# Softmax rows scaled after the values' products, the first attention operands loaded inside the projection phase, and the output projection interleaved with the norm behind it

## The chip, the cores and the metric

The kernel runs on one core of a Trainium2 chip. The metric is the device time of one execution in microseconds (us). Inputs and outputs lie in the chip's memory (HBM); they and nearly all products are float32. A float32 product is made of three TensorE products of rounded parts: each operand is split into a high part (a cast to fp32r) and a low part (the rest), and hi·hi, hi·lo and lo·hi are added in PSUM.

## The reference, cut to what matters

One layer of a streaming encoder, for 1024 prompt frames and for 64 sample frames that continue an older stream with 256 cached frames. Eight heads are RWKV-7 (a recurrence over a matrix state), eight are "FoX" heads: softmax attention with a bias made of running sums of forget gates.

```
mod = silu(c) @ w_ada + b_ada                    # 6 x 1024 columns per sequence
sh1, sc1, gt1, sh2, sc2, gt2 = split(mod, 6)
h    = rms_norm(x, norm1_g) * (1 + sc1) + sh1
proj = h @ w_in                                  # RWKV columns and FoX columns
...                                              # RWKV-7 scan, gate -> y_rwkv
s = einsum(q, k) * HEAD_DIM**-0.5 + (lc_q - lc_k)
p = softmax(where(causal, s, -inf))
y_fox = einsum(p, v)
x  = x + gt1 * (concat([y_rwkv, y_fox]) @ w_out)
h2 = rms_norm(x, norm2_g) * (1 + sc2) + sh2
x  = x + gt2 * ((silu(h2 @ w_ffn_gate) * (h2 @ w_ffn_up)) @ w_ffn_down)
```

Width 1024, 8 RWKV and 8 FoX heads of 64, FFN width 2816. Besides y, the last states, the keys, values and forget gates are outputs.

## The kernel before, in words

Activations stand with their features on the 128 partitions and the frames along the free axis. The frames are cut into two halves: half 0 has the first 512 prompt frames, half 1 the other 512 and the 64 of the sample, 576 in all. Weights come in slices of 128 output columns: `load_w` issues the load (512 KB, four buffers `wraw`), then casts the high part on ScalarE (`whi`) and subtracts the low part (`wlo`, L216) on GpSimd or VectorE. The flag `pool_lo` chooses which.

A scheduler of the framework sets the order of the instructions of each engine from the order in which the program issues them and from which data they need; each engine then runs its own queue strictly in order, and SyncE's queue issues nearly all DMAs.

The stages, by the times of the profile:

- 0 to 40: loads, the first 16 of 48 slices of the `w_ada` product.
- 40 to 680: `phase` for each half: the input projection, slice by slice (`pmm`, L294 to L296), and between the slices the steps of an order that is written out by hand, the string ORDER. Z, D, A, B and N belong to one pair of RWKV heads, Q, K, q, k, V, C and L to FoX heads. B (`rwkv_b`) inverts small triangular matrices (32x32 products, L523, L549), transposes (L567, L575) and then runs the scan, nine dependent steps of 64 frames (L597 to L618). The remaining 32 `w_ada` slices (`pada`, the list `background`) are spread over the projection's slices. Finished queries and keys go by DMA to scratch memory in HBM (`qx`, `kx`), values to `vscr`.
- In half 1, ORDER ends with "Q3 q3 K2 k3 k2 V3". B and N of the last head pair stand in no string; they are issued behind it (`late`).
- 714 to 820 and on to 940: attention, for half 0 and then half 1. `attend` first loads the head's operands from scratch (`qsx`, `k1x`, `q2x`, `k2x`, `vsx`, seven DMAs), then makes units of one or two tiles of 128 queries: scores (`psc`), mask, row maximum (`nm`), exponential with row sum (`p`, `ls`), reciprocal of `ls`, and the multiplication of `p` by it (one tile in three on ScalarE, L917, two on VectorE, L919). Then `p` is transposed (`ppt`), split in two (`pth`, `ptl`), multiplied with the values (`pav`), and the two halves of the partitions are added (`avt`, `fy`, L957 to L959). `Pipe(2)` keeps three units in flight, at different steps. Half 0 has 32 tiles in 16 units, half 1 has 40 tiles in 24 units.
- Between 820 and 940 the output projection of half 0 (`po`, eight slices of `w_out`) is issued between the units of half 1.
- 940 to 1040: first the norm of half 0 is finished and the first part of its FFN input made (`h2_make`, L1040 to L1045), with the output projection of half 1 behind it in program order; then the norm and `h2_make` of half 1. Its residual is L992, its squares L1000 and L1002.
- 1040 to 1490: the FFN's gate and up products (`fast_half`, L1143, seven products in place of eight of half size). From there to the end the down product (`pd`, L1244), which reads the gated activations back from scratch (`act_load`, buffer `as`), splits them (`ah`, `al`) and adds into x.

PSUM has eight banks. `pav` has one buffer in half 0 and in half 1.

Of the kernel before, what the change touches and what calls it, by code (L numbers as in the profile page):

```python
# [7 lines left out]
F32 = mybir.dt.float32  # L8
# [3 lines left out]
ALU = mybir.AluOpType  # L12
# [23 lines left out]
         "T3 Z0 D0 A0 L Z1 K0 D1 U3 B0 A1 D2 Z2 Q0 N0 k0 A2 q0 D3 Q1 B1 K1 q1 Z3 A3 k1 V2 N1 V1 B2 V0 Q2 q2 K3 N2 Q3 q3 K2 k3 k2 V3")  # L36
# [28 lines left out]
class K:  # L65
# [7 lines left out]
    def consts(self):  # L73
# [14 lines left out]
        self.ct = self.cmid.tile([P, KT, 32], F32, name="ct")  # L88
# [570 lines left out]
    def logf(self, hf):  # L659
# [43 lines left out]
        if hf.smp:  # L703
            order += [(5, True, SP, P, None), (6, False, SP + P, P, None), (4, False, SP + PAST, SS, SP)]
# [25 lines left out]
        for g in (order[0:4], order[4:]):  # L730
            if not g:
                continue
            if g[0][0] != 0:
                pr = self.ps([32, 4, P], tag="fx", name="plr")
                rows = self.slot([32, 4, P], F32R, name="lrow", tag="fx")
            for x, (i, _, _, m, _) in enumerate(g):
                nc.tensor.transpose(pr[:, x, 0:m], q4[0:m, i].rearrange("p a h -> p (a h)"), self.ident[0:m, 0:m])
            w = sum(m for _, _, _, m, _ in g)
            rf = rows.rearrange("r x t -> r (x t)")
            nc.vector.tensor_copy(rf[:, 0:w], pr.rearrange("r x t -> r (x t)")[:, 0:w])  # L740
            ck = g[0][2]
            x0, cq, wq = [(x, cq, 512 if x == 0 else m) for x, (_, _, _, m, cq) in enumerate(g) if cq is not None][0]
            for part in range(2):
                r = 16 + 8 * part
                nc.sync.dma_start(self.kx[:, 130 + part, ck:ck + w], rf[r:r + 8, 0:w].bitcast(F32))
                nc.sync.dma_start(self.qx[:, 128 + part, cq:cq + wq],
                                  rf[8 * part:8 * part + 8, x0 * P:x0 * P + wq].bitcast(F32))
# [38 lines left out]
    def put_split(self, src, j, t0, n, is_k):  # L786
# [5 lines left out]
        for x, r in ((hi, 0 if is_k else 64), (lo, 64 if is_k else 0)):  # L792
            m = min(n, 512)
            for h in range(2):
                t = (self.kx if is_k else self.qx)[2 * j + h, r:r + 64]
                hs = slice(64 * h, 64 * h + 64)
# [32 lines left out]
    def cache_kv(self, j):  # L829
# [6 lines left out]
        self.put_split(kf, j, SP, PAST, 1)  # L836
        self.put_v(j, vc, 8, 2, P)

    def att_pools(self, es, R):
# [13 lines left out]
        T2 = lambda name, shape: [ap.tile(shape, F32R, name=f"{name}x{i}") for i in range(2)]  # L853
        self.qs, self.q2 = T2("qs", [P, 640]), T2("q2", [68, 640])
        self.k1, self.k2 = T2("k1", [P, 1344]), T2("k2", [68, 1344])
        self.vs = T2("vs", [P, 11, P])
        for i in range(2):
            nc.gpsimd.memset(self.qs[i][:, 576:640].bitcast(F32), 0.0)
            nc.gpsimd.memset(self.q2[i][:, 576:640].bitcast(F32), 0.0)

    def attend(self, hd, hf):

        nc = self.nc
        j, h = hd // 2, hd % 2
        hs = slice(64 * h, 64 * h + 64)
        i2 = hd % 2
        qs, q2, k1, k2, vs = self.qs[i2], self.q2[i2], self.k1[i2], self.k2[i2], self.vs[i2]
# [12 lines left out]
        else:  # L880
            nc.sync.dma_start(vs[:, 0:4].bitcast(F32), self.vscr[hd][:, 0:4])
        if h == 0:
# [4 lines left out]
        def unit(qp):  # L887
# [4 lines left out]
            ptiles = []  # L892
            for t in range(1 if smp else 2):
# [13 lines left out]
                nc.tensor.matmul(pq[0:qn, nk - qn:nk], self.identb[0:qn, 0:qn], self.cmask[0:qn, 0:qn], start=False,  # L907
                                 stop=True, skip_group_check=True)
                nm = self.tpool.tile([P, 1], F32, tag="nm", name="nm")
                ls = self.tpool.tile([P, 1], F32, tag="ls", name="ls")  # L910
                nc.vector.tensor_reduce(nm[0:qn], pq[0:qn, 0:nk], axis=AX.X, op=ALU.max, negate=True)
                p = self.tpool.tile([P, 1024], F32, tag="p", name="p")
                nc.scalar.activation(p[0:qn, 0:nk], pq[0:qn, 0:nk], AF.Exp, bias=nm[0:qn], accum_out=ls[0:qn])
                nc.vector.reciprocal(ls[0:qn], ls[0:qn])
# [725 lines left out]
```

## Time and profile before

| | us |
|---|---|
| median of three runs | 1759.51 (1754.32 to 1764.12) |
| the profiled execution | 1761.91 |
| its span in the trace | 1760.2 |
| TensorE busy | 1673.6 (95%), mean granted clock 0.974 |
| VectorE busy | 1105.8 (63%) |
| ScalarE busy | 728.0 (41%) |
| GpSimd busy | 267.6 (15%) |

In the profile PE is TensorE, PEld its weight loads, DVE VectorE, ACT ScalarE, POOL GpSimd, SP SyncE, and SPq the issuing of DMAs on SyncE's queue. Lines such as L917 are lines of the kernel before. PEclk is the clock that TensorE was granted, 1.00 being full speed. A row of a stretch gives its bounds and length, then busy time and number of instructions for each engine, then PEclk, the DMA engines' busy share and GB/s. A row of a group gives line, engine, operation, output<-inputs, shape and number, then the sum of the busy time and the mean of one in ns, then the time for which the engine had sat idle ahead of them and what ended that.

### The profile page before, as it was taken

The page shows a single profiled execution, that of the slowest core. Times are in us where ns is not written, and L with a number is a line of the kernel's source. Part 1 is how long each engine was busy: PE and PEld are TensorE (multiplying, and loading weights), DVE is VectorE, ACT ScalarE, POOL GpSimd, SP SyncE. Part 2 cuts the span into 40 slices and gives each one's busy share as a digit, 9 for nine tenths or more (in the row PEclk, how much of TensorE's full clock was granted, in tenths as well). Part 3 has the DMA queues.
Part 4 walks back from the last instruction along what each step waited for, and adds up shares of the span by engine and source line. Part 5 has one row for each costly group of instructions (what it writes and reads, how often), then busy time and mean ns, then how long its engine had stood idle before and what let it go on. Part 6 is the DMA issues. An engine that isn't in the chain of part 4 may idle for free.

```text
span 1760.2 us, 33567 instructions
## 1 busy us (share of the span) xinstructions
PE 1673.6 (95%) x12893; PEld 1454.0 (83%) x12893; DVE 1105.8 (63%) x2518; ACT 728.0 (41%) x1532; POOL 267.6 (15%) x468
## 2 busy tenths in 40 slices
PE   5999999999999998889999779999999999999999
PEld 3676666688888886666888779999999999999998
DVE  6676676757786753777876685556666654444434
ACT  4435454543555344566776363233333222112110
POOL 2102121121222122100212300000000000222221
PEclk9999999999999997889999899999999999999999
DMA  8435356642233336376663302222222224533313
GB/s 314 151 87 157 116 165 195 184 122 71 76 75 92 107 84 167 96 203 166 158 188 128 106 34 83 74 74 74 74 74 78 79 89 134 182 99 93 99 36 120
DMA packets 136143, 207.10 MB, mean 118 GB/s; under 512 B 64687, under 2 KB 72911, under 8 KB 135983
## 3 DMA queue, kind: packets, MB, share of 16 engines
q1 hardware_dynamic: 135982, 204.95, 39.1%
q8 instruction: 102, 1.67, 0.4%
q14 instruction: 59, 0.48, 0.1%
HBM read 157.65 MB, written 47.25 MB: 116 GB/s over the span
## 4 chain that ended last, share of the span: by engine, by line
PE 81%; DVE 7%; ACT 6%; issue 3%; DMA 3%; POOL 1%; SPq 0%; ACTq 0%; DVEq 0%; POOLq 0%
PE pd L1244 15%; PE pfc L1143 7%; PE pfe L1143 7%; PE pfa L1143 7%; PE pmm L294 5%; PE pmm L296 5%; PE pmm L295 5%; PE pfb L1143 4%; PE pav L952 2%; PE pbs L375 2%; PE ppt L930 2%; PE pA L464 2%; PE pS L613 1%; PE po L295 1%; PE po L294 1%
## 5 line engine op out<-in xcount | busy, mean ns | idle before, releaser
L216 POOL TENSOR_TENSOR wlo<-wraw,whi 128x512 fp32r<-128x512 f32 (+2 forms) x64 | 107.1, 1675 | 777.5 <-ACT whi L212 772.2
L294 PE MATMUL pmm<-hhi,whi 128*128 128x288 f32 (+1 forms) x624 | 220.3, 353 | 1.0 <-ACT pb L317 0.7
L295 PE MATMUL pmm<-hlo,whi 128*128 128x288 f32 (+1 forms) x624 | 216.8, 347 | 1.4 <-DVE hlo L272 1.4
L296 PE MATMUL pmm<-hhi,wlo 128*128 128x288 f32 (+1 forms) x624 | 215.6, 345 | 0.0
L212 ACT CAST whi<-wraw 128x1024 fp32r<-128x1024 f32 (+2 forms) x116 | 99.2, 855 | 234.8 <-PE pd L1244 168.1
L1244 PE MATMUL pd<-ah,whi 128*128 128x512 f32 (+1 forms) x528 | 173.3, 329 | 2.2 <-ACT ah L212 2.2
L1244 PE MATMUL pd<-al,whi 128*128 128x512 f32 (+1 forms) x528 | 174.1, 330 | 0.5 <-DVE al L216 0.5
L1244 PE MATMUL pd<-ah,wlo 128*128 128x512 f32 (+1 forms) x528 | 173.7, 329 | 0.0
L1248 DVE SCALAR_TENSOR_TENSOR x1t<-pd,mod,x1t 128x512 f32<-128x512 f32 x192 | 90.6, 497 | 132.1 <-PE pd L1244 131.0
L294 PEld LDWEIGHTS pmm<-hhi,whi 128*128 128x128 f32 x624 | 119.2, 191 | 14.3 <-ACT pb L317 2.5
L295 PEld LDWEIGHTS pmm<-hlo,whi 128*128 128x128 f32 x624 | 119.4, 191 | 11.1 <-DVE hlo L272 2.1
L296 PEld LDWEIGHTS pmm<-hhi,wlo 128*128 128x128 f32 x624 | 119.4, 191 | 10.2 <-issue 1.2
L1143 PE MATMUL pfc<-hh,hS 128*128 128x256 f32 (+1 forms) x352 | 102.3, 291 | 8.0 <-ACT hh L1045 5.6
L1244 PEld LDWEIGHTS pd<-ah,whi 128*128 128x128 f32 x528 | 99.8, 189 | 10.5 <-ACT ah L212 2.7
L1244 PEld LDWEIGHTS pd<-al,whi 128*128 128x128 f32 x528 | 99.8, 189 | 8.5 <-DVE al L216 0.7
L1244 PEld LDWEIGHTS pd<-ah,wlo 128*128 128x128 f32 x528 | 99.9, 189 | 7.5
L604 POOL TENSOR_SCALAR sd<-sv,pc 64x64 f32<-64x64 f32 x136 | 72.1, 530 | 202.7 <-DVE sv L617 190.3
L1143 PE MATMUL pfc<-hl,hS 128*128 128x256 f32 (+1 forms) x352 | 102.4, 291 | 0.0
L1143 PE MATMUL pfc<-hh,lS 128*128 128x256 f32 (+1 forms) x352 | 102.2, 290 | 0.0
L1143 PE MATMUL pfa<-hh,whi 128*128 128x256 f32 (+1 forms) x352 | 102.0, 290 | 0.0
L1143 PE MATMUL pfa<-hl,whi 128*128 128x256 f32 (+1 forms) x352 | 101.8, 289 | 0.0
L1143 PE MATMUL pfa<-hh,wlo 128*128 128x256 f32 (+1 forms) x352 | 101.4, 288 | 0.0
(360 smaller groups left out, 4471.6 us busy)
## 6 DMA issues: line engine op xcount, KB each, us to landing
wraw<-in_w_in_dram SPq DMA_DIRECT2D x52, 512.0 KB
wada<-in_w_ada_dram SPq DMA_DIRECT2D x48, 512.0 KB
as<-actscr SPq DMA_DIRECT2D x22, 544.0 KB
wraw<-in_w_gate_dram SPq DMA_DIRECT2D x22, 512.0 KB
wraw<-in_w_up_dram SPq DMA_DIRECT2D x22, 512.0 KB
wraw<-in_w_down_dram SPq DMA_DIRECT2D x40, 256.0 KB
wraw<-in_w_out_dram SPq DMA_DIRECT2D x16, 512.0 KB
actscr<-sg SPq DMA_DIRECT2D x22, 288.0 KB
```

The lines of the kernel that those rows point to most:

```text
L212: nc.scalar.copy(hi, src)
L216: eng.tensor_tensor(lo, src, hi.bitcast(F32), op=ALU.subtract)
L294: nc.tensor.matmul(ps[0:M, 0:n], whi[:, k, 0:M], xhi[:, k, off:off + n], start=(k == 0), stop=False)
L295: nc.tensor.matmul(ps[0:M, 0:n], whi[:, k, 0:M], xlo[:, k, off:off + n], start=False, stop=False)
L296: nc.tensor.matmul(ps[0:M, 0:n], wlo[:, k, 0:M], xhi[:, k, off:off + n], start=False, stop=(k == kt - 1))
L375: nc.tensor.matmul(ps[:, 0:n], w, x[:, off:off + n], start=True, stop=True)
L464: nc.tensor.matmul(pa[h][:, i], kb[hp, c + i], rk[hp, c + i], start=True, stop=True)
L604: nc.gpsimd.tensor_scalar(sd[hsl[h]], sv[hsl[h], c, h], pc[hsl[h], c], None, op0=ALU.mult)
L930: nc.tensor.transpose(pt[0:rows, b - b0, t * P:t * P + qn], p[0:qn, b * P:b * P + rows], self.ident[0:qn, 0:qn])
L1143: nc.tensor.matmul(ps, l[:, k], r[:, s, k], start=(first and k == 0 and y == 0), stop=(k == 3 and y == 2), skip_group_check=True)
L1244: nc.tensor.matmul(ps[:, 0:n], w[:, i], x[:, t:t + n], start=(i == 0 and y == 0), stop=(i == len(fs) - 1 and y == 2))
L1248: nc.vector.scalar_tensor_tensor(dst, ps[:, so - off:so - off + l], self.mod[:, 40 + o, b:b + 1], dst, op0=ALU.mult, op1=ALU.add)
```

## The change

1. In ORDER, half 1 ends with "Q3 q3 P B3 K2 k3 k2 V3". B3, which ran behind the phase, stands inside it. P is new: it gives back the memory that the RWKV preparation used (`rws`), allocates the attention operands of half 0 there (`att_ops`), and issues the loads of heads 0 and 1, fourteen DMAs (`att_load`).
2. The sample's 64 keys and queries lie directly behind the prompt's and the cache behind those, so `put_split` issues one DMA where it issued two (in half 1).
3. `p` is no longer multiplied by the reciprocals. The two tiles of a unit share one reciprocal; TensorE transposes it, broadcast over the columns, into the second half of the bank of `pav`, and VectorE multiplies `fy` by that. The 72 multiplications of whole tiles and 32 of 72 reciprocals go; 72 transposes and 40 multiplications of 64x256 come.
4. Eight slices of the `w_ada` product (40 to 47, the gate of the FFN) move from the projection to behind the output projection of half 1: four behind its last norm (`x1_rs`), four behind `h2_make` of half 1 (`gap`). The first load of `w_up` moves to `gap` too, and its preparation under the gate product of half 1.
5. In the output projection of half 1, `h2_make` of half 0 is issued one step per slice instead of as a whole ahead of it; the first two slices of `w_out` are loaded and split ahead; from here on the low parts of `w_out` and `w_down` are subtracted on VectorE (`pool_lo = False`), not GpSimd.
6. The first two loads of `as` are issued ahead of the last gate/up product, into buffers of their own; the next two at the start of its last half.

On TensorE, where the projection ends and attention begins, before (`pmm` is the projection, `pg` to `pu` the inversions of the last head pair, `pkbt` and `pvt` its transposes, `pR` the scan's first step):

```order
L295 MATMUL pmm<-hlo,whi 128x288
L296 MATMUL pmm<-hhi,wlo 128x288
L523 MATMUL pg_8390<-gt,At 32x32 x15
L523 MATMUL pw_8431<-g_8389,inv_693 32x32 x9
L523 MATMUL pu_8453<-inv_693,g_8389 32x32 x18
...
L549 MATMUL pu_8516<-inv_693,gt 32x32 x9
L567 MATMUL pkbt<-ident,kb 128x128 x9
L575 MATMUL pvt<-ident,z 128x128 x4
L597 MATMUL pR<-sv,At 128x128
```

The same place after:

```order
L597 MATMUL pR<-sv,At 128x128
L295 MATMUL pmm<-hlo,whi 128x288
L296 MATMUL pmm<-hhi,wlo 128x288
L575 MATMUL pvt<-ident,z 64x128
...
L296 MATMUL pmm<-hhi,wlo 128x288
L814 MATMUL pkv<-ident,fv 128x128 x2
L911 MATMUL psc<-k1x_8027,qsx_8025 128x256
L913 MATMUL psc<-k2x_8028,q2x_8026 128x256
L917 LDWEIGHTS identb
L917 MATMUL psc<-cmask,identb 128x128
L613 MATMUL pS<-sv,kb 128x128
```

The inversions and the first scan step now stand among the projection's products, and the first scores (`psc`) two instructions behind the last of them; the other eight scan steps stand among attention's instructions.

On VectorE, in the output projection of half 1, before (`nsq` squares of half 0's norm, `x_1` half 1's residual, `x_0` and `hl` half 0's FFN input):

```order
L1002 TENSOR_TENSOR nsq<-nsq 128x512 x2
L992 SCALAR_TENSOR_TENSOR x_1_11730<-po,mod,x_1_11730 128x224
L992 SCALAR_TENSOR_TENSOR x_1_11730<-po,mod,x_1_11730 128x64
L1040 SCALAR_TENSOR_TENSOR x_0_9704<-x_0_9704,g_162,nrs 128x512 x8
L992 SCALAR_TENSOR_TENSOR x_1_11730<-po,mod,x_1_11730 128x224
L992 SCALAR_TENSOR_TENSOR x_1_11730<-po,mod,x_1_11730 128x64
L1044 TENSOR_TENSOR hl_11726<-x_0_9704,hh_11725 128x1024
```

and after:

```order
L1013 TENSOR_TENSOR nsq<-nsq 128x512 x2
L1003 SCALAR_TENSOR_TENSOR x_1_11566<-po,mod,x_1_11566 128x224
L1003 SCALAR_TENSOR_TENSOR x_1_11566<-po,mod,x_1_11566 128x64
L216 TENSOR_TENSOR wlo<-wraw,whi 128x1024
L1051 SCALAR_TENSOR_TENSOR x_0_9520<-x_0_9520,g_162,nrs 128x512 x3
L1003 SCALAR_TENSOR_TENSOR x_1_11566<-po,mod,x_1_11566 128x224
L1003 SCALAR_TENSOR_TENSOR x_1_11566<-po,mod,x_1_11566 128x64
L1051 SCALAR_TENSOR_TENSOR x_0_9520<-x_0_9520,g_162,nrs 128x512 x4
L1003 SCALAR_TENSOR_TENSOR x_1_11566<-po,mod,x_1_11566 128x288
```

The subtraction of a weight slice's low part now stands in VectorE's queue, between the squares of half 0's norm and the scaling of its FFN input, and the scaling is cut into pieces with residuals between them.

The core of the diff:

```diff
-"... Q2 q2 K3 N2 Q3 q3 K2 k3 k2 V3"
+"... Q2 q2 K3 N2 Q3 q3 P B3 K2 k3 k2 V3"
...
-            m = min(n, 512)
...
-                nc.sync.dma_start(t[:, t0:t0 + m], x[hs, 0:m].bitcast(F32))
-                if n > m:
-                    c = SP + PAST if is_k else SP
-                    nc.sync.dma_start(t[:, c:c + SS], x[hs, 512:576].bitcast(F32))
+                nc.sync.dma_start(t[:, t0:t0 + n], x[64 * h:64 * h + 64, 0:n].bitcast(F32))
...
-                nc.scalar.activation(p[0:qn, 0:nk], pq[0:qn, 0:nk], AF.Exp, bias=nm[0:qn], accum_out=ls[0:qn])
-                nc.vector.reciprocal(ls[0:qn], ls[0:qn])
-                self.flip = (self.flip + 1) % 3
-                if self.flip == 0:
-                    nc.scalar.activation(p[0:qn, 0:nk], p[0:qn, 0:nk], AF.Copy, scale=ls[0:qn])
-                else:
-                    nc.vector.tensor_scalar(p[0:qn, 0:nk], p[0:qn, 0:nk], ls[0:qn], None, op0=ALU.mult)
+                nc.scalar.activation(p[0:qn, 0:nk], pq[0:qn, 0:nk], AF.Exp, bias=nm[0:qn], accum_out=ls[0:qn, t:t + 1])
                 ptiles.append((p, qn, nk))
             yield 1
+            nt = len(ptiles)
+            nc.vector.reciprocal(ls[0:qn, 0:nt], ls[0:qn, 0:nt])
...
-            pv = self.ps([P, 256], tag="av", name="pav")
+            pv = self.ps([P, 512], tag="av", name="pav")
+            for t in range(nt):
+                nc.tensor.transpose(pv[:, 256 + t * P:256 + t * P + qn], ls[0:qn, t:t + 1].to_broadcast([qn, P]),
+                                    self.ident[0:qn, 0:qn])
...
             nc.vector.tensor_tensor(fy[hs, c:c + nq], pv[hs, 0:nq], tmp[hs, 0:nq], op=ALU.add)
+            nc.vector.tensor_tensor(fy[hs, c:c + nq], pv[hs, 256:256 + nq], fy[hs, c:c + nq], op=ALU.mult)
...
-            self.background = [lambda t=t: self.ada_fin(self.ada_mm(t)) for t in range(16, 48)]
+            self.background = [lambda t=t: self.ada_fin(self.ada_mm(t)) for t in range(16, 40)]
...
+            def early():
+                rws.close()
+                p = E(at0, "att0")
+                self.att_ops([p, p], halves[0])
+                for hd in range(2):
+                    self.att_load(hd, halves[0])
...
+            self.pool_lo = False
             acc = None
             for o in range(KT):
                 acc = self.x1_sq(halves[0], o, acc)
-            for _ in self.h2_make(halves[0], self.x1_rs(halves[0], acc)):
-                pass
+            w1 = [self.load_w(A["w_out"][o], [P, KT, P]) for o in range(2)]
+            h2 = self.h2_make(halves[0], self.x1_rs(halves[0], acc))
...
-                self.outproj(halves[1], o, ("ab", "ce")[o % 2])
+                self.outproj(halves[1], o, ("ab", "ce")[o % 2], w1[o] if o < 2 else None)
                 acc = self.x1_sq(halves[1], o, acc)
+                next(h2, None)
+                if o in (0, 2):
+                    next(h2, None)
...
-            raw.append(self.fast_raw(pair("w_up")))
+            ada = [(t, self.ada_load(t)) for t in range(40, 44)]
             rs = self.x1_rs(halves[1], acc)
...
+            def gap():
+                ada_run(ada[4:])
+                raw.append(self.fast_raw(pair("w_up")))
+            ada_run(ada)
+            ada += [(t, self.ada_load(t)) for t in range(44, 48)]
...
+            def early():
+                h2s[2].close()
+                self.spool.pools["as"] = L(early_s, "sas0", 2)
+                for f in range(2):
+                    pre.append(self.act_load(f, None))
```

More of the change, by code (lines that the diff above doesn't have):

```diff
@@ L703, in logf @@
         if hf.smp:
-            order += [(5, True, SP, P, None), (6, False, SP + P, P, None), (4, False, SP + PAST, SS, SP)]
+            order += [(5, True, SP + SS, P, None), (6, False, SP + SS + P, P, None), (4, False, SP, SS, SP)]
         acc = self.lacc
@@ L732, in logf @@
                 continue
-            if g[0][0] != 0:
+            g = sorted(g, key=lambda e: e[2])
+            if g[0][2] != hf.t0:
                 pr = self.ps([32, 4, P], tag="fx", name="plr")
                 rows = self.slot([32, 4, P], F32R, name="lrow", tag="fx")
-            for x, (i, _, _, m, _) in enumerate(g):
-                nc.tensor.transpose(pr[:, x, 0:m], q4[0:m, i].rearrange("p a h -> p (a h)"), self.ident[0:m, 0:m])
+            ck = g[0][2]
+            prf, rf = pr.rearrange("r x t -> r (x t)"), rows.rearrange("r x t -> r (x t)")
+            for i, _, c, m, _ in g:
+                nc.tensor.transpose(prf[:, c - ck:c - ck + m], q4[0:m, i].rearrange("p a h -> p (a h)"),
+                                    self.ident[0:m, 0:m])
             w = sum(m for _, _, _, m, _ in g)
[L739 to L742, printed above, removed]
+            nc.vector.tensor_copy(rf[:, 0:w], prf[:, 0:w])
+            cq = g[0][4]
+            wq = sum(m for _, _, _, m, c in g if c is not None)
             for part in range(2):
@@ L881, in attend @@
             nc.sync.dma_start(vs[:, 0:4].bitcast(F32), self.vscr[hd][:, 0:4])
+    def attend(self, hd, hf):
+        nc = self.nc
+        j, h = hd // 2, hd % 2
+        hs = slice(64 * h, 64 * h + 64)
+        qs, q2, k1, k2, vs = self.ops[hf.i][hd % 2]
+        n, t0 = hf.n, hf.t0
+        if hd > 1 or hf.smp:
+            self.att_load(hd, hf)
         if h == 0:
@@ L1157, in fast_half, with ffn @@
                 h(x)
-    def ffn(self, halves, raw, w, h2gen, mid):
+    def ffn(self, halves, raw, w, h2gen, gap, early, mid):
         nc, A = self.nc, self.A
@@ L1168, in ffn @@
             p, up = i // 2, i % 2
-            if i + 2 < len(src):
+            if i and i + 2 < len(src):
                 raw.append(self.fast_raw(src[i + 2]))
+            if i == len(src) - 2:
+                early()
             old, nw = gen, {}
-            gen = self.fast_prep(raw[i + 1], nw) if i + 1 < len(src) else iter(())
+            gen = self.fast_prep(raw[i + 1], nw) if 0 < i < len(src) - 1 else iter(())
             for hf in halves:
@@ L1197, in out, with prep @@
                                           sg[hf.i][:, 2 * q - 2:2 * q].rearrange("p q t -> p (q t)"))
-                hooks = [lambda x: next(gen, None) if self.STEPS[hf.i][x] else None]
+                def prep(x):
+                    for _ in range((0, 0, 0, 3, 2, 2, 1)[x] if i == 0 else self.STEPS[hf.i][x]):
+                        next(gen, None)
+                hooks = [prep]
                 if hf.i == 0:
@@ L1209, in ffn @@
                         pass
+                    gap()
+                    raw.append(self.fast_raw(src[2]))
+                    gen = self.fast_prep(raw[1], nw)
             w = nw
@@ L1302, in phase @@
                 self.cache_kv(j)
+            elif op == "P":
+                self.early()
             elif op == "S":
@@ L1433, in run @@
             self.spool.pools.update({"fs": L(mix0, "sfs", 2)})
+            self.att_ops([R(att, f"attp{i}", 1) for i in range(2)], halves[1])
             PB = lambda es, name, b: E(es, name, b, space=PSUM, reuse_waits="tile")
```

100 lines of the change are left out of this document (55 added, 45 removed).

## The prediction

> **What bounds the kernel now.** I read the busy times first, then the slices, then a table of the stages, and last the places where TensorE's share falls.
>
> ```profile
> span 1760.2 us, 33567 instructions
> PE 1673.6 (95%) x12893; PEld 1454.0 (83%) x12893; DVE 1105.8 (63%) x2518; ACT 728.0 (41%) x1532; POOL 267.6 (15%) x468
> PE   5999999999999998889999779999999999999999
> PEclk9999999999999997889999899999999999999999
> ```
>
> TensorE is busy 95% of the span, so work taken off another engine pays only where TensorE waits. The slices show where: slices 16 to 18 (about 700 to 830 us; TensorE's share and its clock fall) and slices 22 and 23 (970 to 1055). The stages, cut at these places:
>
> ```profile
> core 0: us, PE busy (x) PEld busy (x) DVE busy (x) ACT busy (x) POOL busy (x), PEclk, DMA share, GB/s
> 40.00:680.00 640.00, 622.61 (x5484) 491.62 (x5484) 437.63 (x1181) 305.34 (x685) 126.33 (x278) 0.98 0.43 121
> 679.00:695.00 16.00, 11.93 (x233) 9.44 (x232) 3.89 (x12) 7.66 (x20) 6.29 (x12) 0.67 0.56 158
> 679.00:714.00 35.00, 27.05 (x284) 21.04 (x283) 9.63 (x35) 11.09 (x34) 9.81 (x20) 0.58 0.50 133
> 679.00:779.00 100.00, 84.13 (x606) 62.70 (x605) 63.13 (x200) 56.82 (x176) 19.02 (x58) 0.83 0.52 143
> 714.00:779.00 65.00, 57.08 (x323) 41.65 (x323) 53.50 (x166) 45.73 (x142) 9.21 (x38) 0.96 0.53 149
> 780.00:820.00 40.00, 34.82 (x155) 25.48 (x155) 26.32 (x49) 22.12 (x45) 3.01 (x5) 0.83 0.80 221
> 820.00:940.00 120.00, 119.20 (x728) 97.67 (x726) 89.54 (x189) 82.52 (x186) 25.09 (x36) 1.00 0.55 150
> 940.00:1013.00 73.00, 59.80 (x421) 58.05 (x421) 52.26 (x69) 36.07 (x49) 24.40 (x7) 0.93 0.40 134
> 1013.00:1040.00 27.00, 17.35 (x106) 15.95 (x106) 23.36 (x35) 22.32 (x35) 0.00 (x0) 0.87 0.01 1
> 1478.00:1500.00 22.00, 19.25 (x121) 17.76 (x120) 11.78 (x18) 6.43 (x7) 1.82 (x1) 0.93 0.87 280
> ```
>
> The projection (40:680) is TensorE's: 97% busy, clock 0.98. Behind it come 100 us (679:779) that hold the last RWKV pair and the attention of half 0: 35 us at a mean clock of 0.58, then 65 us in which TensorE and VectorE are busy 88% and 82%, so that each waits for the other. 820:940 is full. The output projection of half 1 (940:1013) has 13 us idle. FFN and down product, outside the table, are TensorE's.
>
> **The change, part by part.** A: eight `w_ada` slices leave the projection.
>
> ```profile
> 40.00:434.00 394.00, 34.48 (x543) 18.50 (x543) 4.93 (x31) 8.26 (x31) 0.97 0.49 141
> ```
>
> This row holds only the instructions of that product: 34.48 us for 32 slices, 1.08 each. Eight are 8.6 us off TensorE in a stage that it bounds: -8.6. They come back in the gap of G below. SyncE's 32 missing DMA issues lie beside this stage, whose TensorE is full without them: 0.
>
> B: the inversions, transposes and first scan step of the last pair move in front of the projection's end. There they need 11.93 us at a clock of 0.67, that is 8.0 us at full clock, of which about 1 is other work (`pkv`) that stays. They now lie among products that fill TensorE: +7. Below: +3, if they fall into the 17 us that the stage 40:680 leaves idle; above: +11.9, the busy time as it stands. P issues fourteen DMAs on SyncE ahead of the inversions' own loads; the projection's products cover that.
>
> C: what is left of the 100 us.
>
> ```profile
> 679.12 0.29 PE L296 MATMUL pmm<-hhi,wlo 128*128 128x288 f32 x1
> ...
> 694.66 0.77 PE L597 MATMUL pR<-sv,At 128*128 128x128 f32 x2 [0.92 <-ACT sv L578]
> ...
> 699.37 0.77 PE L597 MATMUL pR<-sv,At 128*128 128x128 f32 x2 [0.36 <-DVE sv L617]
> 705.48 0.77 PE L902 MATMUL psc<-k1x,qsx 128*128 128x256 f32 x2
> 779.01 0.36 PE L952 MATMUL pav<-ptl,vsx 128*128 128x256 f32 x1
> 700.88 0.34 SPq L881 DMA_DIRECT2D vsx<-vscr  x1
> ```
>
> The last product of the projection starts at 679.12, the first score only at 705.48, behind operand loads that SyncE issues until 700.88; between them the scan runs alone, a step every 4.7 us. After, the scores stand two instructions behind the last `pmm`, with eight scan steps among them, and their operands are loaded already. So the stage becomes one attention stage from the first microsecond, and VectorE's and TensorE's work sets its length:
>
> ```profile
> L944 DVE TENSOR_TENSOR ptl<-ppt,pth 128x256 fp32r<-128x256 f32 (+2 forms) x40 | 16.6, 417 | 2.0 <-ACT pth L943 1.8
> L919 DVE TENSOR_SCALAR p<-p,ls 128x128 f32<-128x128 f32 (+3 forms) x22 | 8.5, 388 | 0.3
> L959 DVE TENSOR_TENSOR fy<-pav,avt 64x256 f32<-64x256 f32 x15 | 6.3, 417 | 1.6 <-ACT avt L957 1.4
> L914 DVE RECIPROCAL ls<-ls 128x1 f32<-128x1 f32 x31 | 4.8, 159 | 2.3 <-ACT p L913 1.8
> ```
>
> VectorE has 63.13 us in 679:779. Off it go the prologue's 3.89, the 22 multiplications of `p` (8.5) and half of 32 reciprocals (16 x 0.159 = 2.5); 16 multiplications of `fy` come, 16 x 0.417 = 6.7 by the addition beside them. That leaves 54.9. At the 82% at which VectorE ran in 714:779 it takes 67 us. ScalarE loses ten multiplications and stays below VectorE. The other side: TensorE had 57.08 us at clock 0.96 there, 54.8 at full clock; three more scan steps of ten products and 32 reciprocal transposes come. What a transpose costs stands here (the first row seven of them):
>
> ```profile
> 871.63 1.07 PE L930 MATMUL ppt<-ident,p 128*128 128x128 f32 x7
> 872.46 0.36 PE L952 MATMUL pav<-pth,vsx 128*128 128x256 f32 x1
> L930 PE MATMUL ppt<-ident,p x137: 222/272/329, 840.2 to 920.0; 128*128 128x128 f32 x122, 64*128 64x64 f32 x10, 64*64 64x64 f32 x5
> ```
>
> The next product starts 0.83 us after the first of seven, 0.12 us each; I take 0.1 for transposes and scan products alike: 3.2 + 3.0. That makes 61 us, 90% of 67. I take 68, one for filling the pipe: -32. Below: at 100% VectorE 55 us, -45. Above: at 70% 79 us, -21.
>
> The Trainium skill, "TensorE: Matmul & The Clock Gate", Part 4, speaks against the added transposes: it puts a 128x128 one at about 275 ns and says that transposes do not count as busy time for the clock. By 275 ns the 32 would take 8.8 us instead of 3.2, C would be -26. The median of 272 ns is the trace's too, but seven took 0.83 us together, so it is a duration, not a cost; what the rule would do through the clock is weighed among the rivals.
>
> D: the changeover (780:820) starves TensorE by 5 us and runs at clock 0.83, with the DMA engines busy 80%. Operands of half 1 have memory of their own and can come earlier, in fewer pieces; but the stage ahead is shorter. -3, between 0 and -8. E: attention of half 1 gets 40 transposes in 820:940 and just ahead of it, where TensorE is full: 40 x 0.1 = +4; below +2, above +7, where VectorE's 24 multiplications, 10 us, delay a bank's release.
>
> F: the output projection of half 1.
>
> ```profile
> 960.68 9.27 issue
> 969.99 9.28 POOL wlo L216
> 979.31 0.61 PE po L296
> ...
> PE po L296 <- POOL wlo L216: 10.2, 2, 8.8
> L216 DVE TENSOR_TENSOR wlo<-wraw,whi 128x1024 fp32r<-128x1024 f32 x50 | 61.0, 1219 | 23.9 <-ACT whi L212 23.0 <-DMA dm<-At 0.6
> L1002 DVE TENSOR_TENSOR nsq<-nsq 128x512 f32<-128x512 f32 (+1 forms) x14 | 14.1, 1009 | 5.6 <-ACT nsq L1000 5.6
> L992 DVE SCALAR_TENSOR_TENSOR x<-po,mod,x 128x288 f32<-128x288 f32 (+3 forms) x25 | 10.0, 423 | 15.5 <-PE po L296 15.5
> ```
>
> A low part on GpSimd sits in the chain with 9.28 us and keeps TensorE waiting for 10.2; on VectorE it takes 1.22. That wait goes. But the new order queues the next low part behind the squares of half 0's norm and pieces of its scaling, on an engine that is busy 52.26 of 73 us already; six to eight low parts add 7 to 10. VectorE's queue then holds 60 to 62 us, and slice 3 waits some 9 us for its low part where GpSimd's wait was. So most of the gain is given back: 69 us for 73, -4. Below: VectorE packs, 61 us, -12. Above: the residual (15.5 us of waiting for `po` now) falls behind the scaling and holds PSUM, +5.
>
> G: the gap of 27 us (1013:1040), in which TensorE is busy for 17, takes the eight `w_ada` slices, 8.6 us. Their last step is VectorE's and ScalarE's work, 8 x (4.93 + 8.26)/31 = 3.4 us on engines that this gap waits for (23.36 and 22.32 of 27), and `w_up` is loaded later. +2, between -2 and +5.
>
> H: FFN to down.
>
> ```profile
> 1479.99 5.29 DMA as<-actscr
> ...
> 1487.77 6.46 DMA as<-actscr
> 1495.40 14.64 PE pd L1244 x75
> ```
>
> The loads are in the chain with 11.8 us, but most of that is covered: in 1478:1500 TensorE is idle for 2.75 us and loses 1.5 to the clock of 0.93. Issued earlier they no longer show: -3.5, between 0 and -4.3. Down's 40 low parts on VectorE and FFN's other stages lie beside a full TensorE: 0.
>
> Sum: -8.6 + 7 - 32 - 3 + 4 - 4 + 2 - 3.5 = -38. The profiled execution took 1761.91 us, 1.7 more than its span, so 1724 for it; it stands 2.4 over the median of the three runs, 1759.5, so 1722 against that. What a measurement tells from no change is about 0.5%, 9 us.
>
> **The rivals.** R1, attention of half 0 stays bound by latency. Every unit passes the one `pav` bank, which is now held for the transposes and one more VectorE instruction, 0.1 x 2 + 0.42 = 0.6 us; were that in line for all 16 units, it is 10 us, and scan steps that wait in VectorE's queue at their 4.7 us each would stretch the first 38. The stage then takes 84 us, not 68: 1738. For it: 88% and 82% busy now, so neither engine is the bound alone. Against: `p` no longer waits for its own reciprocal. A chance of 0.18.
>
> R2, better than summed: C packs near 90% (61 us, -7) and the stall of F vanishes (-8): 1707. For it: 820:940 runs TensorE at 99%. Against: there it has `po` products to fill with, and here none. 0.1.
>
> R3, slower than before: the clock of TensorE does not recover in half 0's attention. 679:714 shows 0.58 where TensorE was 77% busy with short dependent products, and the scan's eight steps and the transposes now lie inside attention. The 61 us of TensorE work take 122 at half clock, 54 more: 1776. It decides for slower where the stage outlasts 106 us (68 + 38), a mean clock under 0.58. Against it: 714:779 is attention with the last four of nine scan steps in it (by their spacing from 694.66), at 0.96, and the 122 transposes of 128x128 in 840:920 lie in a stage at 1.00. The rule above would work in this way, and these rows don't bear it out. 0.05.
>
> R4, the moves do little: the early loads wait for the memory that P gives back, and the first scores come where they came (26 us behind the last `pmm`), while the scan runs alone until then. C brings only VectorE's saving, 8.5 + 2.5 - 6.7 = 4.3, at 82% 5 us; with F and G at their worse ends the sum is -8.6 + 7 - 5 - 3 + 4 + 5 + 5 - 3.5 = +1: 1760. For it: SyncE's queue is in order, and a load that waits in it holds all behind it. Against: behind P four steps of the projection (K2 k3 k2 V3) still follow, in which a late load can catch up. 0.07.
>
> **How the numbers follow.** My forecast has 0.6, R1 0.18, R2 0.1, R3 0.05, R4 0.07. The bounds of C alone (-45 to -21) reach from 1709 to 1733; with F's on top, from 1701 to 1742. The range, 1703 to 1746, takes in R1 and R2, and leaves out R3 and R4, 0.12, and the corner where C and F both come out at their best. Faster: 0.6 + 0.18 + 0.1 = 0.88; R4 lies within 0.5%, 0.07; slower 0.05.
>
> **What would show it.** In the trace after: from the last `pmm` to half 0's last `pav` 64 to 72 us with clock above 0.9 (C; 80 or more speaks for R1, a first score over 10 us behind the last `pmm` for R4, a clock under 0.6 for R3); the last `pmm` at about 677 us (A and B: 679.1 - 8.6 + 7); no L216 on GpSimd behind attention, and TensorE waiting once, for some 9 us, for a low part on VectorE (F); the `as` loads out of the chain (H). I am wrong above all if VectorE's share in the stage of half 0 is not near 82%.

## The result: 0.6% faster, where 2.1% was forecast

The changed kernel takes 1747.72 us (median of twelve runs, 1745.18 to 1755.71), the kernel before 1759.17 beside it (twelve runs): a ratio of 0.9942, 95% interval [0.9923, 0.9961]. The forecast was 1722, its range ended at 1746. A second set of runs of the same kernel (the control below) gave 0.9951 [0.9932, 0.9969]. The ratios below are each against the kernel before, run beside it; one run of the kernel with few small products (1768.9 us, at a granted clock of 0.962 where its others have 0.975 to 0.986) is left out of its ratio as a slow one.

The page of the changed kernel, busy times and slices:

```profile
span 1750.6 us, 33374 instructions
PE 1680.4 (96%) x12965; PEld 1461.3 (83%) x12965; DVE 1115.5 (64%) x2534; ACT 713.0 (41%) x1508; POOL 178.3 (10%) x412
PE   6999999999999999979999989999999999999999
PEclk9999999999899999989999989999999999999999
```

The two gaps of TensorE are narrower, and yet its busy time has grown from 1673.6 to 1680.4 us: the eight slices of `w_ada` have only moved, and 72 transposes have come. The stages after, cut at the same events as before:

```profile
core 0: us, PE busy (x) PEld busy (x) DVE busy (x) ACT busy (x) POOL busy (x), PEclk, DMA share, GB/s
36.00:698.00 662.00, 642.18 (x5559) 508.91 (x5560) 441.51 (x1184) 312.72 (x698) 128.77 (x281) 0.96 0.42 116
698.00:771.00 73.00, 61.55 (x409) 49.48 (x408) 56.56 (x171) 46.17 (x148) 16.08 (x55) 0.96 0.56 165
771.00:937.00 166.00, 160.62 (x909) 124.70 (x910) 108.66 (x220) 92.69 (x215) 23.70 (x40) 0.94 0.57 158
937.00:1003.00 66.00, 59.84 (x418) 57.36 (x418) 50.67 (x74) 34.19 (x48) 1.43 (x1) 0.97 0.43 144
1003.00:1031.00 28.00, 20.97 (x194) 17.95 (x193) 20.36 (x40) 23.95 (x42) 0.00 (x0) 0.83 0.37 124
1470.00:1500.00 30.00, 30.00 (x203) 28.31 (x203) 20.83 (x34) 9.66 (x11) 0.00 (x0) 1.00 0.86 300
```

The events are starts of first and last products, which each tile's row names as "first to last start". Before and after for the projection, the values' products and the output projection:

```profile
L296 PE MATMUL pmm<-hhi,wlo x624: 288/297/796, 34.9 to 679.1; 128*128 128x288 f32 x104, 128*128 128x512 f32 x52
L952 PE MATMUL pav<-ptl,vsx x184: 273/282/388, 719.1 to 935.8; 128*128 128x256 f32 x160, 128*128 128x64 f32 x16, 64*128 64x64 f32 x8
L296 PE MATMUL po<-mixfh,wlo x96: 289/296/598, 806.3 to 1010.5; 128*128 128x288 f32 x64, 128*128 128x512 f32 x32
```

```profile
L296 PE MATMUL pmm<-hhi,wlo x624: 289/298/798, 37.0 to 698.2; 128*128 128x288 f32 x104, 128*128 128x512 f32 x52
L962 PE MATMUL pav<-ptl,vsx x184: 272/283/461, 707.6 to 936.5; 128*128 128x256 f32 x160, 128*128 128x64 f32 x16, 64*128 64x64 f32 x8
L296 PE MATMUL po<-mixfh,wlo x96: 289/296/629, 799.1 to 1002.7; 128*128 128x288 f32 x64, 128*128 128x512 f32 x32
```

The last product of the projection starts at 698.2; before it was 679.1, and the forecast was 677. From such starts come all stage lengths below, one profile each (us; "clock" is the projection's loss, the sum of 1 - PEclk over pieces of 1 us; PEclk of the whole stretch, rounded to two places, would give 26 for 23.4, and some of the expectations below use that):

| kernel | projection | clock | attention, half 0 | attention, half 1 | output projection, half 1 | to FFN's end | down | span |
|---|---|---|---|---|---|---|---|---|
| before | 644.8 | 11.9 | 99.9 | 156.8 | 74.7 | 479.2 | 266.9 | 1760.2 |
| before again | 644.5 | 12.8 | 100.3 | 157.8 | 74.2 | 479.1 | 262.8 | 1757.5 |
| changed | 662.2 | 23.4 | 72.2 | 166.1 | 66.2 | 481.9 | 262.5 | 1750.6 |
| changed, control | 658.9 | 20.1 | 72.1 | 166.3 | 66.2 | 482.2 | 262.5 | 1747.5 |
| slices back | 660.4 | 20.1 | 69.9 | 163.6 | 66.2 | 479.2 | 262.0 | 1740.2 |
| B3 late | 651.1 | 21.8 | 84.5 | 163.2 | 66.0 | 480.9 | 262.5 | 1746.9 |
| softmax as before | 660.6 | 20.5 | 72.6 | 156.6 | 66.4 | 481.7 | 262.5 | 1740.5 |
| both back | 655.8 | 15.4 | 69.7 | 158.3 | 66.3 | 479.0 | 261.9 | 1731.6 |
| both back, B3 late | 643.8 | 13.7 | 84.8 | 156.5 | 67.5 | 479.0 | 261.9 | 1732.4 |
| slices alone moved | 652.4 | 23.6 | 101.9 | 158.6 | 74.5 | 480.1 | 263.0 | 1769.0 |

Between the first two profiles, attention of half 0 and output projection gave 27.7 + 8.5 us, the down product 4.4; the projection took 17.4 back, half 1's attention 9.3, the stretch to FFN's end with the gap in it 2.7, the start 1.7. In all 9.6, the spans' difference. Two profiles of one kernel differ too: the changed kernel's two by 3.3 us in the projection, nearly all of it clock, and those of the kernel before by 4.1 in the down product.

### The profile page after: what moved, and what is told of

Same layout as the page of the kernel before. It is cut to its first block, busy times and chain, and to the rows that moved or that the text cites. A ratio compares the mean times of both kernels' runs of the same rounds, so it can differ in the third digit from the quotient of the medians.

```text
span 1750.6 us, 33374 instructions
## 1 busy us (share of the span) xinstructions
PE 1680.4 (96%) x12965; PEld 1461.3 (83%) x12965; DVE 1115.5 (64%) x2534; ACT 713.0 (41%) x1508; POOL 178.3 (10%) x412
## 4 chain that ended last, share of the span: by engine, by line
PE 84%; DVE 6%; ACT 5%; DMA 3%; issue 2%; SPq 0%; DVEq 0%; ACTq 0%
PE pd L1265 15%; PE pfc L1154 7%; PE pfe L1154 7%; PE pfa L1154 7%; PE pmm L294 5%; PE pmm L296 5%; PE pmm L295 5%; PE pfb L1154 4%; PE pav L962 2%; PE pbs L375 2%; PE ppt L936 2%; PE pA L464 2%; DMA wada<-in_w_ada_dram 2%; PE po L296 2%; PE po L294 2%
## 5 line engine op out<-in xcount | busy, mean ns | idle before, releaser
L296 PE MATMUL pmm<-hhi,wlo 128*128 128x288 f32 (+1 forms) x624 | 219.4, 352 | 0.0
L216 DVE TENSOR_TENSOR wlo<-wraw,whi 128x1024 fp32r<-128x1024 f32 (+2 forms) x108 | 103.8, 961 | 25.5 <-ACT whi L212 25.2
L1154 PE MATMUL pfa<-hl,whi 128*128 128x256 f32 (+1 forms) x352 | 101.9, 289 | 0.0
```

The source lines that it names most:

```text
L216: eng.tensor_tensor(lo, src, hi.bitcast(F32), op=ALU.subtract)
L296: nc.tensor.matmul(ps[0:M, 0:n], wlo[:, k, 0:M], xhi[:, k, off:off + n], start=False, stop=(k == kt - 1))
L1154: nc.tensor.matmul(ps, l[:, k], r[:, s, k], start=(first and k == 0 and y == 0), stop=(k == 3 and y == 2), skip_group_check=True)
```

## The experiments

**The slices back in the projection.**

```diff
-            self.background = [lambda t=t: self.ada_fin(self.ada_mm(t)) for t in range(16, 40)]
+            self.background = [lambda t=t: self.ada_fin(self.ada_mm(t)) for t in range(16, 48)]
...
-            ada = [(t, self.ada_load(t)) for t in range(40, 44)]
...
-                ada_run(ada[4:])
...
-            ada_run(ada)
-            ada += [(t, self.ada_load(t)) for t in range(44, 48)]
```

> The changed kernel, with the eight w_ada slices (40 to 47) back in the projection; nothing else undone. In the profile of the changed kernel the stretch from the first to the last product of the input projection took 662.5 us instead of 645.1, with clock losses of some 26 us instead of 12. Theory 1 (the slices were cover: without them TensorE falls idle in half 1 and the clock is halved for a while): the stretch comes to 657 to 661 us with four or five dips of the clock, the gap behind the output projection is 6 to 8 us shorter, and the whole about 1740 us. Theory 2 (the dips have nothing to do with the slices): the stretch grows by the slices' 8.6 us to about 671, the gap shrinks by 6 to 8, the whole stays at 1748 to 1751.

Measured: 1740.4 us (four runs), a ratio of 0.9896 [0.9872, 0.9919]; the control beside it 1749.4. Theory 1 has the stretch and the whole, but not for its reason, and the gap shrank by 3.0 us, not 6 to 8: the projection takes 660.4 us and loses 20.1 of them to the clock, just as the control (658.9, 20.1).

```profile
35.00:695.00 660.00, 641.87 (x5693) 507.43 (x5692) 445.19 (x1200) 314.48 (x705) 130.96 (x281) 0.97 0.44 123
```

So with B3 in the phase the eight slices cost the projection next to nothing. In these two profiles the gain lies behind it: 3.0 us of the gap, and 2.2 in half 0 and 2.7 in half 1, where the clock's loss falls from 2.4 to 0.3 and from 9.5 to 6.5 us. That the slices cause those two falls is not shown: half 0's attention takes 70.5 and 70.2 us, with 0.6 and 0 lost, in two profiles below that have the slices out ("The low parts on GpSimd" and the first swap of D1 and U3).

**B3 behind the phase again** (ORDER without B3, with P).

> The changed kernel with B3 taken out of ORDER again (it runs behind the phase as before); P and its early loads stay. Theory 1 (the moved inversions and the first scan step cost the phase about 7 us and no more, the rest of the 17 us is the clock): the stretch of the projection falls by 7 to about 655, and the stretch from its last product to half 0's last product with the values grows from 72 to 82 to 88 us, because the early operands let attention start beside the inversions: in all 1751 to 1757. Rival (the moved part and the fourteen loads ahead of it stretch the phase by the whole 17): it falls to about 646, the whole comes to 1742 to 1748.

Measured: 1748.1, 0.9927 [0.9900, 0.9955]: no difference from the control. The projection's 651.1 lies between the theories, half 0's 84.5 in theory 1's range, the whole at the edge of the rival's. Without B3 in the phase half 0 is already 15 of the 28 us shorter than before, by the early operands and the rest of the change; B3 brings the other 12 and costs 8 to 11 in the projection.

**The softmax as before.**

```diff
+                nc.vector.reciprocal(ls[0:qn, t:t + 1], ls[0:qn, t:t + 1])
+                self.flip = (self.flip + 1) % 3
+                if self.flip == 0:
+                    nc.scalar.activation(p[0:qn, 0:nk], p[0:qn, 0:nk], AF.Copy, scale=ls[0:qn, t:t + 1])
+                else:
+                    nc.vector.tensor_scalar(p[0:qn, 0:nk], p[0:qn, 0:nk], ls[0:qn, t:t + 1], None, op0=ALU.mult)
...
-            nc.vector.reciprocal(ls[0:qn, 0:nt], ls[0:qn, 0:nt])
...
-            for t in range(nt):
-                nc.tensor.transpose(pv[:, 256 + t * P:256 + t * P + qn], ls[0:qn, t:t + 1].to_broadcast([qn, P]),
-                                    self.ident[0:qn, 0:qn])
...
-            nc.vector.tensor_tensor(fy[hs, c:c + nq], pv[hs, 256:256 + nq], fy[hs, c:c + nq], op=ALU.mult)
```

> The changed kernel with the softmax as before: p is multiplied by its reciprocals, no transposes of sums, no multiplication of fy. Theory 1 (in half 0 VectorE bounds, so the multiplications cost; in half 1 TensorE is full, so the transposes cost, 0.2 us each with the breaks they make): half 0's attention 72 -> 76 to 78 us, half 1's stretch (last values product of half 0 to that of half 1) 166 -> 158, in all 1744 to 1746. Rival (the transposes cost 0.1 us, half 1's 9 us come from its start, where the operands are late): half 0 76 to 78, half 1 162 to 166, in all 1749 to 1753.

Measured: 1741.4, 0.9895 [0.9878, 0.9911], 8.0 below the control and below what either theory said. Half 1 gets shorter by 9.7 us, more than theory 1's 8; half 0 gains nothing from the new form (72.6 against 72.1). Both theories had VectorE as half 0's bound, and both are wrong there.

**The control.**

> The changed kernel once more, unchanged, to see which dips of the clock stay where they are from one execution to the next. Theory 1 (dips belong to the order of the instructions): projection stretch 660 to 665 us with the dips again at about 400 and 465 to 480 us, whole 1748. Theory 2 (they come and go by chance): the stretch differs by more than 5 us from 662.5, or the dips lie elsewhere.

Measured: 1749.4 (1746.8 to 1754.4). Mixed: the dip behind 460 us is there again, the one at 407 is not, one at 540 is new. Some dips stay in place, others come and go, with the same instructions.

**Fewer small products.** The 18 or 36 products of 32 columns in a row of blocks are one product of 288 columns for each row of blocks.

> The changed kernel with the inversions' 32x32 products left out but for one in each row of blocks: 18 products of 32 columns become one of 288, made with the first block's operand, so y and the states are not the reference's. In five profiles so far, dips of the clock stand behind dense runs of these products while TensorE is busy without a gap. Theory 1 (the clock gate takes such a run for idleness): the dips at 141, 290, 345, 460 and 540 to 630 us go, the projection's stretch loses 12 to 17 us of clock beside 8 to 15 us of products: 633 to 642 us instead of 659 to 662. Rival (the dips follow waits elsewhere, the runs only stand by): the stretch loses the products alone, 644 to 652, and the dips stay within 10 us of where they were.

The kernel leaves out most of the inversions' products, so its y and states are not the reference's. Measured: 1742.0 (seven runs, 1732.5 to 1768.9), 0.9897 [0.9865, 0.9929]. The length, 646.7, falls in the rival's range; the places speak for theory 1: no dip between 302 us and the projection's end, none at 345, 460 or 540 to 630. Those at 144 and 290 stayed. The clock's loss is 11.1 us instead of 20.1 and 23.4, so of the 12 to 16 us that the stretch is shorter, 9 to 12 are clock and only the rest the products.

**The slices alone moved**, on the kernel before.

> The kernel before with one part of the change, eight w_ada slices behind the output projection of half 1 (with the load of w_up and its preparation behind them). Theory 1 (the slices cost the phase some 4 us of TensorE, but without them the scheduler packs the inversions of half 1 with one or two projection products between them, and the clock dips at about 460 us): the projection's stretch stays at 643 to 652 us (645 before), the gap grows by 2 to 4, in all 1759 to 1768. Rival (a slice moved is 1.08 us saved): the stretch falls to 636 to 638, in all 1752 to 1754.

Measured: 1767.0 (ten runs), 1.0056 [1.0041, 1.0072]: slower by 9 us. This part of the change alone loses. The projection takes 652.4 instead of 644.8, with 23.6 us of clock loss instead of 11.9. Two stretches of this kernel:

```profile
400.00:420.00 20.00, 18.75 (x129) 16.49 (x131) 15.20 (x36) 7.56 (x19) 4.50 (x9) 0.83 0.20 64
460.00:480.00 20.00, 19.63 (x292) 16.47 (x285) 10.93 (x22) 6.33 (x18) 5.37 (x7) 0.74 0.14 41
```

In the first TensorE idles for 1.25 us where slices stood before; in the second it is busy 98%, and the clock is down to 0.74 all the same.

**Both undone** (slices and softmax).

> The changed kernel with two parts undone together, the w_ada slices back in the projection and the softmax as before. If the two losses are independent (9.0 and 8.0 us against the control): 1730 to 1734. If both are the same few dips of the clock, the second undoing brings little: 1738 to 1741.

Measured: 1732.1 (1729.8 to 1735.5), 0.9853 [0.9825, 0.9881]: the losses add. This version beats both kernels, by 1.5% and, by the ratios, 1.0%.

**The low parts on GpSimd** (without `self.pool_lo = False`).

> The changed kernel with the low parts of w_out (half 1) and w_down on GpSimd again, the interleaved order and the two slices split ahead kept. Theory 1 (GpSimd's 9 us in the chain are what the order gives back to TensorE): the stretch from the last product with the values to the last of the output projection grows from 66.2 to 72 to 76 us, in all 1754 to 1758. Rival (interleaving and the early slices do it, VectorE's low parts only move the wait): 64 to 68, in all 1747 to 1750.

Measured: 1754.7 (ten runs), 0.9984 [0.9970, 0.9999], output projection 71.8: 0.2 short of theory 1's range, and the whole within it. The move to VectorE brings 5.6 of the 8.5 us there; the other 3 belong to the order and the two early slices, which were not parted.

**Both undone, and B3 late.**

> The kernel of the last study with w_ada slices and softmax as before (1732 us), and B3 behind the phase again; P's early operands stay. Theory 1 (B3 in the phase is worth little: its 8 us of TensorE and its dips return there what attention saves): stretch of the projection 655.8 -> 643 to 648, half 0's attention 69.7 -> 80 to 85, in all 1732 to 1738. Rival (B3 inside is most of the 28 us that the stage lost): half 0's attention 92 or more, in all 1745 or more.

Measured: 1736.0 (1734.1 to 1738.9): theory 1. The projection is back at 643.8, half 0 at 84.8. With the slices in, B3 inside costs the projection 12 and saves attention 15. Whether the whole gains is open: the medians differ by 3.9 us, the two profiles by 0.8, and the intervals of the ratios (0.9853 and 0.9886) overlap.

**Full-size products among the small ones.**

```diff
+                        k += 1
+                        if k % 3 == 0:
+                            nc.tensor.matmul(pf[h][:, 384:512], self.identr, self.identr, start=True, stop=True)
```

> The changed kernel with added work: behind every third of the inversions' 32x32 products one more product of 128x128 with 128 columns, of an identity with itself into unused PSUM (36 for each of eight inversions, about 0.07 us each, 20 us in all). Theory 1 (runs of 32x32 products look idle to the clock gate): with full-size products among them the dips behind the runs at about 460, 540 and 620 us go, the clock's loss in the projection's stretch falls from 20 to 26 us to 13 or less. Rival (the dips follow from something else at these places): the loss stays at 20 us or more, and the stretch grows by the 20 us of products.

Measured: 1896.1 (one run), a projection of 806.8 us with 115.6 us of clock loss. Neither theory had this: the loss did not fall, and the stretch grew by 145 to 148 us, not by the 20 of the added products. Of these, 92 to 95 are lost clock. TensorE's instructions in a run of it (`identr` the added product):

```profile
530.13 0.33 PE L531 MATMUL pg<-identr 128*128 128x128 f32 x1
530.39 0.31 PE L528 MATMUL pg<-gt,At 32*32 32x32 f32 x6
530.62 0.33 PE L531 MATMUL pg<-identr 128*128 128x128 f32 x1
530.88 0.31 PE L528 MATMUL pg<-gt,At 32*32 32x32 f32 x6
531.12 0.33 PE L531 MATMUL pg<-identr 128*128 128x128 f32 x1
```

The next instruction starts 0.26 us after each added product and 0.23 after six small ones, at full clock; in an unbroken run 36 small ones take 0.76 (in the rows of the changed kernel below), so six 0.13, and a 128x128 transpose in a row of seven took 0.12. By these, each change of size costs an estimated 0.10 to 0.14 us in which TensorE counts as busy; each added product also loads 128 columns of weights of its own, 0.19 us long in this trace, and the run does not part the two. Stretches with many changes fall to half clock.

**The kernel before, a second profile.**

> The kernel before, for a second profile of it. Theory 1 (the order of the instructions decides at about 460 us): no dip there again, and a projection stretch of 643 to 649 us. Theory 2 (chance): a dip of 3 us or more at 455 to 480 us, or a stretch over 652.

Measured: 1759.2; no dip at 455 to 480, projection 644.5: theory 1. The same place in its first profile and in the changed kernel, one block each:

```profile
455.00:465.00 10.00, 10.00 (x280) 8.98 (x279) 9.47 (x16) 4.51 (x13) 3.64 (x7) 1.00 0.24 61
465.00:475.00 10.00, 9.42 (x65) 6.85 (x63) 6.41 (x14) 4.42 (x14) 2.03 (x4) 1.00 0.18 56
```

```profile
460.00:470.00 10.00, 10.00 (x238) 8.59 (x237) 8.61 (x16) 2.26 (x7) 2.64 (x4) 0.76 0.08 28
470.00:480.00 10.00, 10.00 (x63) 8.38 (x62) 2.32 (x6) 2.21 (x5) 2.25 (x5) 0.56 0.17 54
```

TensorE is busy throughout in the changed kernel, more than before, but at 0.76 and 0.56 of its clock: 6.8 us lost in 20. Part of that run in the changed kernel:

```profile
461.51 0.40 PE L296 MATMUL pmm<-hhi,wlo 128*128 128x288 f32 x1
461.84 0.76 PE L523 MATMUL pg<-gt,At 32*32 32x32 f32 x36
462.52 0.40 PE L294 MATMUL pmm<-hhi,whi 128*128 128x288 f32 x1
462.76 0.29 PE L295 MATMUL pmm<-hlo,whi 128*128 128x288 f32 x1
462.98 0.72 PE L523 MATMUL pw<-g,inv 32*32 32x32 f32 x17
```

Behind the first of these pieces one to four of the projection's products stand between them; in the kernel before it is four to eight.

**The order against the slices' absence.** Two entries of ORDER change places, D1 and U3.

> The changed kernel with two entries of ORDER swapped in half 1, 'K0 U3 D1 B0' for 'K0 D1 U3 B0'; the slices stay out of the projection. In its order the first inversions of half 1 stand in six pieces with 19, 6, 11, 3 and 4 other products between them, ten changes of size; the changed kernel has eight pieces with 13, 1, 2, 2, 1, 3 and 4 between, fourteen changes, and six profiles of that order had a dip of 3 to 7 us there, five of the kernel before's ten changes none. Theory 1 (the order of the pieces makes the dip): no dip at 450 to 480 us, projection stretch 652 to 657 us, in all 1742 to 1746. Rival (the slices' absence makes it): a dip there as before, stretch 658 to 663, in all 1747 to 1751.

> The changed kernel with the softmax as before and the same swap in ORDER. Theory 1: the two gains add, 1741 less 3 to 7: 1734 to 1738. Rival: 1739 to 1743.

> The kernel of 1732 us (slices back in the projection, softmax as before) with the same swap in ORDER; here it makes the run denser, seven pieces with 13, 5, 5, 1, 1 and 3 other products between, twelve changes instead of ten. Theory 1 (the order makes the dip): a dip of 3 us or more at 450 to 480 us although the slices are in, in all 1734 to 1738. Rival (the slices' presence prevents it): none, 1730 to 1734.

Measured: 1746.0 (ten runs, 1737.4 to 1756.2; 0.9928 [0.9901, 0.9954]), 1742.7 (0.9905 [0.9869, 0.9940]) and 1742.2 (0.9904 [0.9870, 0.9938]). The first keeps a dip, 3.4 us at 464 to 471, so the looser order doesn't take it away, as the rival said; its length of 656.3 is theory 1's. The second brings nothing (rival). The third, slices in and order denser, has a dip of 1.7 us there and one of 5.1 at 543, and is 10 us slower than without the swap; its projection loses 25.3 us to the clock instead of 15.4. So neither theory holds as it stands. What stands: with the slices out all eight profiles with the inversions as they are have a dip of 3.4 to 6.8 us that begins at 460 to 466, with them in five of six have none there. Why, the runs don't settle.

## Why the prediction was wrong

**A, the slices (-8.6), is the step that failed.** It took 34.48 us for 32 slices as what their removal saves. That is the time in which any of their instructions ran, each product 273 ns long and overlapped by its neighbours. Projection less idle time less clock loss is 622 us with the slices back (660.4 - 18.2 - 20.1) and 619 in both profiles of the changed kernel; for the kernel before it is 615, and 610 with the slices alone moved; in the last two swaps it is 616 without the slices and 622 with them. So the slices take some 3 to 6 us, not 8.6. And the whole phase lost 7 to 12 us more to the clock than before, which no term and no rival held. Moved alone the slices made the phase 7.6 us longer, by 12 us more of clock loss; with B3 inside, taking them out changed the loss by 0 to 5 us (20.1 and 23.4, slices back 20.1; softmax as before 20.5, both back 15.4). What makes the dips is open.

**B, the moved inversions (+7)** cost 8 to 12 us (658.9 and 662.2 less 651.1; 655.8 less 643.8), up to the bound that was given as the worst. Without idle time and lost clock it is 9 to 10.

**C, half 0's attention (-32)** came to -27.7, 72 us for 68, and the first score starts 0.3 us behind the last `pmm`. But the reason was half wrong: the early start paid, VectorE's saving brought nothing. Half 0's attention with the slices back, new softmax, and then with the old one too:

```profile
696.00:766.00 70.00, 59.18 (x405) 46.91 (x403) 56.56 (x172) 45.43 (x148) 15.97 (x54) 0.99 0.57 168
```

```profile
693.00:763.00 70.00, 60.46 (x374) 45.75 (x373) 59.88 (x195) 50.95 (x158) 16.82 (x54) 1.00 0.57 168
```

With 3.3 us more on VectorE and 5.5 more on ScalarE, the old form fits into the same 70 us; VectorE simply runs at 86% instead of 81%. The 82% of before was no ceiling. TensorE's longest waits there, new form and then old, say how many us in all, how often and the longest:

```profile
PE pav L956 <- DVE fy L970: 2.6, 2, 1.8
PE pav L956 <- DVE ls L926: 2.0, 2, 1.3
```

```profile
PE psc L911 <- ACT p L922: 3.6, 9, 0.6
```

The new form no longer waits as long for `p`, but for the one `pav` bank and for the reciprocal. That is the mechanism of R1, with 4.6 us for its 10 and 72 for its 84; what sets the 70 us is not shown. R4 did not occur, nor did R3: the clock was 0.96. (By C's own rule that the longer of two engines sets the stage, 8.8 us for the transposes instead of 3.2 would have made 66.6 us on TensorE, still under 67, so C would not have become -26.) The sign that was to tell above all, VectorE's share near 82%, came out at 77% (56.56 of 73 us) and told nothing of the miss, which lay ahead of that stage.

**D and E (-3, +4)** came to +9.3 together. With the softmax as before the stage takes 156.6, as it did: D is nothing. The new form costs 5.3 us (163.6 - 158.3) to 9.7 (166.3 - 156.6); without lost clock it is 5.6 and 5.3, and the rest of the 9.7 is a clock loss of 9.5 against 5.1. The idle time is the same 6.2 us in the first pair, so the cost is TensorE's busy time, and the bank's later release, E's worse case, is not what costs. The transposes come in groups of one or two, between products of other shapes:

```profile
854.59 0.33 PE L936 MATMUL ppt<-ident,p 64*128 64x64 f32 x2
854.85 0.43 PE L956 MATMUL pav<-ident,ls 128*128 128x128 f32 x2
855.04 0.36 PE L962 MATMUL pav<-pth,vsx 128*128 128x256 f32 x1
```

These two take 0.19 us to the next start; all 40 of half 1 with the slices back take 4.3, or 0.11 each. So E's price was nearly right. What it missed is about 1 us around them and a clock loss that differs from profile to profile.

**F (-4)** was better, -8.5. The wait for a low part on VectorE exists, but of 2.3 us, not 9:

```profile
962.72 0.40 PE L294 MATMUL po<-mixrh,whi 128*128 128x288 f32 x1 [0.61 <-ACT whi L212]
...
965.80 0.40 PE L296 MATMUL po<-mixrh,wlo 128*128 128x288 f32 x1 [2.30 <-DVE wlo L216]
```

**G (+2)** came as worked out, +2.7. **H (-3.5)** came to -4.4 against the first profile, and in 1470:1500 above TensorE is busy without a gap at a clock of 1.00. But that agreement is luck: the second profile of the kernel before has the loads as late and loses next to nothing there.

```profile
1478.00:1500.00 22.00, 21.59 (x147) 20.04 (x145) 12.99 (x22) 6.35 (x8) 1.82 (x1) 1.00 0.82 278
```

TensorE is idle for 0.41 us where it was 2.75, and the down product takes 262.8 us to the changed kernel's 262.5 (263.0 with the slices alone moved). H is worth some 0.3 to 0.5 us by these; the rest of the 4.4 was a wait of one execution, the one from whose profile the forecast was made.

By the first two profiles A and B were 19 us too hopeful, D and E 8, C 4; F gave 4.5 back and H 0.9, G took 0.7, and the projection started 1.7 us later. By the second profile of each kernel it is 16, 7.5 and 4, with 4 back from F, 3 too hopeful in H and 1 in G. The range missed because it was made of C's bounds and F's, and no rival lay in the projection, which counted as settled at 97% busy.

## What to carry to other kernels

The busy time of a group of short, overlapping products is not what their removal saves on an engine that is full; a profile with the group taken out or moved alone tells it, and here it was about half, with a clock loss beside it. Work that is taken off a busy engine pays only if the engines that then set the stage get nothing for it: here VectorE gave 3.3 us in half 0 that nobody waited for, and TensorE took 40 transposes in half 1, where it was full. A stretch that is 97% busy can still lose time in its clock: sum 1 - PEclk by stage beside the idle time, before and after, over short pieces. And a wait read from one profile may be that execution's alone: a second profile of the kernel before would have shown it for H.

## What the runs showed of the hardware

The clock's losses come in steps of 1.7 us: 1.7, 3.4, 5.1 and 6.8 are the sizes of nearly all dips of these traces, read from stretches of 1 us. The Trainium skill, "TensorE: Matmul & The Clock Gate", Part 1, says that the clock is either half or full, and judged over free-running windows of some 3.4 us; half of 3.4 is 1.7, and the trace agrees. Not expected was that a dip needs no idle time that the trace shows: in the eight profiles with a dip that begins at 460 to 466 us, TensorE showed as busy for 7.86 to 8.00 of the 8 us ahead of it, in runs of 32x32 products among full-size ones. The same page's section "Why this matters for your kernels" advises against idle gaps of over some 3 us; these dips of 3.4 to 6.8 us had none ahead of them. With most of the small products left out they were gone, and added full-size products, one for every three small ones, made the loss far worse (115.6 us instead of 20.1 and 23.4). Such runs alone don't make a dip: in 455:465 of the kernel before TensorE is busy throughout with 280 products, and the clock stays at 1.00.
